# Mixer 1 of a two-layer hybrid backbone: second copies of context keys on VectorE, a dummy exponential, a query product placed inside the first attention, and norm steps pinned in TensorE's order

## The chip, the cores and the metric

The kernel runs on one core of one Trainium2 chip. TensorE (PE) multiplies matrices, VectorE (DVE), ScalarE (ACT) and GpSimd (POOL) work on their results, and SyncE (SP) and the others start DMA transfers. The metric is the device time of one execution in microseconds (us). Times are given as the median of several runs; the profile is that of one further execution, with its own time.

## The reference

A stream of 512 latent tokens and one of 256 context tokens, 1024 wide, pass two layers. Each layer is half a feed-forward network (FFN, SwiGLU, 2816 wide), a token mixer, and again half an FFN; each of these is modulated (scale and shift from a conditioning vector) and closed by a LayerNorm over the 1024 features of a token. The change lies in the mixer of the second layer, "mixer 1", and in the norm that closes the FFN ahead of it. Cut to what matters:

```
def layer_norm(x, g, b):
    mu = mean(x); var = mean(square(x - mu))
    return (x - mu) * rsqrt(var + LN_EPS) * g + b

def window_gqa(u_lat, u_ctx, w_qkv, w_o, sinks, with_ctx_out):
    # 16 query heads, 4 key/value heads, 64 wide; 512 latent rows in 4 blocks of 128; 256 context rows
    q = axial_rope(u_lat @ w_q) * scale          # (512, 16 heads, 64)
    k = axial_rope(u_lat @ w_k)                  # (512, 4 heads, 64)
    v = u_lat @ w_v
    kc, vc = u_ctx @ w_k, u_ctx @ w_v            # context keys: no rotation
    for b in range(4):                           # block of 128 queries against 3 blocks of keys
        s_win = where(|pos_q - pos_k| <= 128, q_b . k[b-1..b+1], -1e30)
        s_ctx = q_b . kc
        p = softmax([s_win, s_ctx, sink])        # sink: a logit per head without a value
        o_b = p_win @ v[b-1..b+1] + p_ctx @ vc
    return o @ w_o
```

Inputs and output are fp32.

## The kernel before, in words

**Precision.** Activations lie transposed: 1024 features in 8 tiles (k = 0 to 7) of 128 partitions, tokens along the free axis; columns 0 to 511 are latent tokens, 512 to 767 context. A matrix product is made of three products of the reduced type fp32r: each operand is a high part and the rest. `mm3` issues them: high by high (line 163), high by low (L165), low by high (L166). A weight quarter of 128x512 is split as it arrives: ScalarE makes the high part `wh` (L102), GpSimd the rest `wl` (L104). The modulated activations are `uh` and `ul` (L319, L321 and L323 on ScalarE, with a subtraction on VectorE).

**What sets the order.** Each engine runs its instructions in a fixed order and waits by semaphores for the others. The program text gives an order; the tile framework's scheduler, started with a timeline simulation (L1549), then reorders each engine's instructions within what their data allow. Two devices in the text steer it. `behind(x, y)` makes x stand after y on the same engine, without a wait. `plan(point=[steps])` puts steps into an agenda, and `at(point)` runs them at that point of the text: this is how the eight steps of a LayerNorm are spread over the product loop that comes next. `layer_norm(..., firm=True)` adds one more tie: the matmul after the variance product is put behind it, through the variable `in_front`, which `mm3` reads once and clears.

**The norm ahead of mixer 1** is called l3 and has a latent part l3[0] and a context part l3[1]. Its steps are sums, mean (matmul `pml`), centers (subtraction, squares on ScalarE L460, sums to `aql` on VectorE L356), variance (`pvl`, four or two small matmuls, L476), reciprocal root, spreading (`prl`, L404), and the last scaling and modulation. The steps of l3[1] are hung into mixer 1's first product loop at the points wa_3, wa_6 and wq0_0_4.

**Mixer 1** (`wa_mixer`) begins with one loop over the eight k tiles: for each k four value products `vw` (128x256, for four blocks of 128 tokens) and two key products `wk` (128x512, two key heads each) and the point `wa_k`. The key products are copied out with a scale (`qek`, L1125 on ScalarE) and rotated by `turned`: a matmul with a rotation matrix (`prk`, L1131), two VectorE operations (L1133, L1135) and one on GpSimd (L1134). `stack_k` then writes each key head into two tiles, so that high and low parts lie in the two halves of the partitions: a copy to its own half (L869, ScalarE), a copy to the other half (L870, ScalarE), the difference (L871, VectorE), and a copy of the difference (L872, ScalarE). It does this for the 512 latent columns and, later, for the 256 context columns (product `wkc`). Query products are `wq{u}_{i}` (u = 0 to 3, i = 0 or 1, two heads each; 8 k, so 24 products of 128x512); they are copied out with the scale (`qeq`, L1125), rotated (`prq`, L1131) and stacked by `stack_q` (L862 on ScalarE, L863 on VectorE). The text has this order: query 0_0, key rotations, query 0_1, rotation of query 0_0, context keys 0, rotation of query 0_1, context keys 1, context values (`vw_4` and `vw_5`), query 1_0, and then the attention of head pair 0.

**Attention** (`attn`) goes over four blocks of 128 queries. For each block and each of two heads the scores against the window (`sw`) and the context (`sc`) are two matmuls each (L877 high, L878 low part of the keys). VectorE adds the mask and takes the minimum (scores are negated) in two passes (L1221, L1224). ScalarE makes the exponentials with their sums (L1236, L1238, L1240). VectorE adds the sink's share (L1246 or L1249) and takes the reciprocal (L1250); GpSimd scales by it (L920). PE transposes the probabilities (`tpw`, `tpc`, L901), which are copied out, and multiplies them with the values (`wo`, L911). The points wm{s}_{b} and wo{s}_{b} lie after the transposes and at the end of block b of head pair s. After head pair 0 query 1_0 is rotated, and after head pair 1 query 1_1 is made.

## Time and profile before

| | |
|---|---|
| median of 3 runs | 2719.22 us (2715.05 to 2722.56) |
| profiled execution | 2723.84 us, its span 2722.1 us |
| mean granted TensorE clock | 0.991 |
| instructions | 47725 |
| PE busy, 0 to 2060 us | 2015.00 us, clock 1.00 |
| PE busy, 2060 to 2066 us | 6.00 us, clock 1.00 |
| PE busy, 2066 to 2122 us (start of mixer 1) | 51.72 of 56.00 us, clock 0.94 |
| PE busy, 2122 to 2722 us | 559.85 of 600.00 us, clock 0.98 |

The span runs from the first to the last instruction of the profiled execution; its time includes what lies around that. In the rows of the timeline the first number is the instruction's start in us from the span's start, the second its duration (of a group of xN together), then the engine, the line and operation, output and inputs, shapes, and in brackets the time for which the engine had stood idle before it and the instruction that ended the wait. In the rows of stages the first number after the window is its length; then come the busy times of PE, of the weight load, of VectorE, ScalarE and GpSimd, each with its count of instructions, and at the end PE's granted clock (1.00 is full), the DMA share and GB/s. Names lose their numbers there: `wq` is any of the query products, `sw` any window score.

### The profile page before, as it was taken

What the parts mean: (1) busy time and instruction counts of PE and PEld (TensorE: products, weight loads), DVE (VectorE), ACT (ScalarE), POOL (GpSimd) and SP (SyncE); (2) the same over time, 40 slices, a digit from 0 to 9 for tenths busy, and PEclk for the clock granted to TensorE, in tenths of its full rate; (3) what the DMA queues carried; (4) which work ended last, traced back from release to release, by engine and by line L of the source; (5) the groups of instructions that cost most, each with busy time, mean ns of one, the idle gap of its engine ahead of it and who ended that gap; (6) DMA issues with size and microseconds to landing.
All of it is one profiled execution on the core that took longest, in us unless ns stands there. A gap on an engine that the chain in (4) does not pass through costs nothing.

```text
span 2722.1 us, 47725 instructions
## 1 busy us (share of the span) xinstructions
PE 2632.6 (97%) x16858; PEld 2406.2 (88%) x16858; DVE 1835.4 (67%) x4268; ACT 1206.5 (44%) x2505; POOL 1666.3 (61%) x1515
## 2 busy tenths in 40 slices
PE   8999999999999899999999999999999998999997
PEld 5899998888888889999998899999987777899997
DVE  4977778775545687656565766666667776687765
ACT  5334343266455444443432534333327655554542
POOL 4786766455433566967664578676645544667762
PEclk9999999999999999999999999999999999999998
DMA  9367565522221213444453225546642111245551
GB/s 331 101 181 204 139 164 141 146 78 80 59 59 53 69 47 94 120 125 128 120 137 102 77 78 151 146 126 189 179 148 65 32 32 43 67 106 128 136 146 57
DMA packets 295758, 311.90 MB, mean 115 GB/s; under 512 B 27872, under 2 KB 194016, under 8 KB 294496
## 3 DMA queue, kind: packets, MB, share of 16 engines
q1 hardware_dynamic: 279104, 279.36, 35.0%
q0 software_dynamic: 16128, 29.37, 6.4%
q8 instruction: 133, 2.18, 0.3%
q14 instruction: 105, 0.86, 0.1%
q10 hardware_dynamic: 288, 0.14, 0.0%
HBM read 300.92 MB, written 12.25 MB: 115 GB/s over the span
## 4 chain that ended last, share of the span: by engine, by line
PE 55%; DVE 6%; ACT 1%; DMA 1%; issue 1%; POOL 0%; SPq 0%; DVEq 0%; ACTq 0%; POOLq 0%
PE pd0b L163 2%; PE pd0b L165 2%; PE pd0b L166 2%; PE pd1a L163 2%; PE pd1a L165 2%; PE pd1a L166 2%; PE wo L911 1%; DMA wr<-in_wst_dram 1%; PE pd1b L163 1%; PE pd1b L165 1%; PE pd1b L166 1%; DVE z L504 1%; PE tpw L901 1%; DVE sw L1221 1%; PE wq L163 0%
## 5 line engine op out<-in xcount | busy, mean ns | idle before, releaser
L104 POOL TENSOR_TENSOR wl<-wr,wh 128x512 fp32r<-128x512 f32 x200 | 261.9, 1327 | 148.4 <-ACT wh L102 95.2
L104 POOL TENSOR_TENSOR wl_s<-S,wh_s 128x512 fp32r<-128x512 f32 x240 | 318.1, 1361 | 54.4 <-ACT wh_s L102 53.9
L102 ACT CAST wh_s<-S 128x512 fp32r<-128x512 f32 x256 | 155.6, 621 | 426.9 <-POOL S L645 138.7
L645 POOL TENSOR_TENSOR S<-wr,wr 128x512 f32<-128x512 f32 x128 | 174.1, 1360 | 187.8 <-DMA wr<-in_wst_dram 165.4
L212 DVE CUSTOM_DVE_ANT_0 jk<-wt,cb 128x512 f32<-128x512 f32 x360 | 244.8, 680 | 21.6 <-DMA wt<-in_wmodt_dram 17.5
L104 POOL TENSOR_TENSOR wl_a<-wr,wh_a 128x512 fp32r<-128x512 f32 x144 | 190.0, 1366 | 19.3 <-ACT wh_a L102 16.9
L102 ACT CAST wh_a<-wr 128x512 fp32r<-128x512 f32 x192 | 119.1, 622 | 150.7 <-PE pd1b L165 19.4
L102 ACT CAST wh<-wr 128x512 fp32r<-128x512 f32 x200 | 120.8, 617 | 98.6 <-DMA wr<-in_wst_dram 18.9
L504 DVE SCALAR_TENSOR_TENSOR z<-pd0b,gt,z 128x256 f32<-128x256 f32 (+1 forms) x168 | 96.9, 594 | 39.3 <-PE pd0b L166 39.1
L504 DVE SCALAR_TENSOR_TENSOR z<-pd1a,gt,z 128x512 f32<-128x512 f32 (+1 forms) x150 | 88.9, 605 | 40.2 <-PE pd1a L166 39.1
L920 POOL TENSOR_SCALAR p<-p,l 128x512 f32<-128x512 f32 x64 | 44.5, 698 | 100.6 <-DVE l L1027 93.5
L504 DVE SCALAR_TENSOR_TENSOR z<-pd0a,gt,z 128x512 f32<-128x512 f32 (+1 forms) x160 | 93.8, 612 | 16.5 <-PE pd0a L166 16.2
L645 POOL TENSOR_TENSOR S<-wr,S 128x512 f32<-128x512 f32 x64 | 90.6, 1415 | 3.4
L645 POOL TENSOR_TENSOR S<-S,wr 128x512 f32<-128x512 f32 x64 | 90.1, 1408 | 2.9
L920 POOL TENSOR_SCALAR pw<-pw,l 128x512 f32<-128x512 f32 (+1 forms) x64 | 42.8, 670 | 72.2 <-DVE l L1250 42.2
L340 POOL TENSOR_SCALAR z<-z,ag_None,ab_None 128x256 f32<-128x256 f32 (+1 forms) x69 | 52.3, 762 | 51.7 <-DVE uh L325 32.6
L1026 ACT ACTIVATE p<-s,m 128x512 f32<-128x512 f32 x64 | 44.0, 689 | 77.8 <-DVE m L1023 73.4
L326 DVE TENSOR_TENSOR ul<-ufl,uh 128x256 fp32r<-128x256 f32 (+1 forms) x88 | 59.6, 685 | 6.1 <-ACT uh L321 3.1
L504 DVE SCALAR_TENSOR_TENSOR z<-pd1b,gt,z 128x512 f32<-128x512 f32 (+1 forms) x91 | 53.2, 618 | 10.0 <-PE pd1b L166 9.7
L319 ACT ACTIVATE ufl<-z,bi_None,sc_None 128x256 f32<-128x256 f32 (+1 forms) x77 | 48.1, 638 | 25.6 <-DVE z L489 25.2
L104 DVE TENSOR_TENSOR wl_a<-wr,wh_a 128x512 fp32r<-128x512 f32 x48 | 52.3, 1101 | 5.7 <-ACT wh_a L102 5.4
L163 PE MATMUL vn<-wh,uh 128*128 128x256 f32 x192 | 54.7, 285 | 1.1 <-DVE nq L863 0.6
(1483 smaller groups left out, 10583.5 us busy)
## 6 DMA issues: line engine op xcount, KB each, us to landing
wr<-in_wst_dram SPq DMA_DIRECT2D x456, 256.0 KB
wt<-in_wmodt_dram SPq DMA_DIRECT2D x206, 256.0 KB
wr_0b<-in_wst_dram SPq DMA_DIRECT2D x47, 256.0 KB
wr_1b<-in_wst_dram SPq DMA_DIRECT2D x47, 256.0 KB
wr_2b<-in_wst_dram SPq DMA_DIRECT2D x47, 256.0 KB
wr_3b<-in_wst_dram SPq DMA_DIRECT2D x47, 256.0 KB
wm<-in_wmod_dram SPq DMA_DIRECT2D x8, 1024.0 KB
zspare<-in_wmodt_dram SPq DMA_DIRECT2D x30, 256.0 KB
```

The lines of the kernel that those rows point to most:

```text
L102: nc.scalar.copy(hi[:], src[:])
L104: x = eng.tensor_tensor(out=lo[:], in0=src[:], in1=hi[:].bitcast(F32), op=ALU.subtract)
L163: behind(nc.tensor.matmul(ps, a[0], b[0], start=first, stop=False), in_front[0])
L165: nc.tensor.matmul(ps, a[0], b[1], start=False, stop=False)
L166: last_pe[0] = nc.tensor.matmul(ps, a[1], b[0], start=False, stop=last)
L212: x = nc.vector.tensor_tensor_reduce(out=junk[:], in0=w[:], in1=cb[st], scale=1.0, scalar=0.0, op0=ALU.mult, op1=ALU.add, accum_out=out[st])
L319: nc.scalar.activation(uv, zs, AF.Identity, scale=s1, bias=s2)
L326: return hi, nc.vector.tensor_tensor(out=lo, in0=uv, in1=uo.bitcast(F32), op=ALU.subtract)
L340: nc.gpsimd.tensor_scalar(out=zs, in0=zs, scalar1=prm[2][:, d:d + 1], scalar2=prm[3][:, d:d + 1], op0=ALU.mult, op1=ALU.add)
L504: last[0] = nc.vector.scalar_tensor_tensor(out=zt(d, c0, c1), in0=pd, scalar=gt[:, d, st:st + 1], in1=zt(d, c0, c1), op0=ALU.mult, op1=ALU ...
L645: nc.gpsimd.tensor_tensor(out=t[:], in0=a[:], in1=b[:], op=o)
L920: nc.gpsimd.tensor_scalar(out=p, in0=p, scalar1=r, scalar2=0.0, op0=ALU.mult, op1=ALU.add)
```

## The change

The change has four parts. One: for the context columns, `stack_k` makes the second copy (other half, L870) on VectorE and not on ScalarE. Two: after the copies out of the keys, an exponential of two columns of `nsink` (the negated sink logits, an input that is loaded at the start) is written to a small tile that nothing reads. Three: the product of query 1_0 is no longer in the text ahead of the attention but at the point wm0_0, in the first block of head pair 0, after that block's transposes. Four: a flag `sticky`, set at the point wa_6 and cleared at wq0_1, keeps `in_front` from being cleared, so that every product triple that is issued in between is put behind the norm's small matmul (L476 or L404 by which was last); and the last steps of l3[1] move from wq0_0_4 to wq0_0_7.

```diff
--- before.py
+++ after.py
@@ -157,11 +157,11 @@
         for f in agenda.pop(point, ()):
             f()
 
-    in_front = [None]
+    in_front, sticky = [None], [False]
 
     def mm3(ps, a, b, first, last):
         behind(nc.tensor.matmul(ps, a[0], b[0], start=first, stop=False), in_front[0])
-        in_front[0] = None
+        in_front[0] = in_front[0] if sticky[0] else None
         nc.tensor.matmul(ps, a[0], b[1], start=False, stop=False)
         last_pe[0] = nc.tensor.matmul(ps, a[1], b[0], start=False, stop=last)
 
@@ -863,11 +863,11 @@
             nc.vector.scalar_tensor_tensor(out=q[lo, c0:c1], in0=src[hi, :], scalar=scale, in1=q[hi, c0:c1].bitcast(F32),
                                            op0=ALU.mult, op1=ALU.subtract)
 
-    def stack_k(k0, k1, kl0, kl1, c0, c1, src):
+    def stack_k(k0, k1, kl0, kl1, c0, c1, src, both=False):
 
         for k, kl, own, other in ((k0, kl0, LOW, HIGH), (k1, kl1, HIGH, LOW)):
             nc.scalar.copy(k[own, c0:c1], src[own, :])
-            nc.scalar.copy(k[other, c0:c1], src[own, :])
+            (nc.vector.tensor_copy if both else nc.scalar.copy)(k[other, c0:c1], src[own, :])
             nc.vector.tensor_tensor(out=kl[own, c0:c1], in0=src[own, :], in1=k[own, c0:c1].bitcast(F32), op=ALU.subtract)
             x = nc.scalar.copy(kl[other, c0:c1], kl[own, c0:c1].bitcast(F32))
         return x
@@ -1154,6 +1154,7 @@
             at(f"wa_{k}")
         ks = [[slab(f"wk{x}_{i}") for x in ("0", "1", "l0", "l1")] for i in range(2)]
         kes = [scaled(f"k{i}", kp[i], 1.0) for i in range(2)]
+        nc.scalar.activation(small("le", "le_w"), nsink[:, 0:2], AF.Exp)
         vt = []
         for j in range(4):
             vt.append(vtile(f"vtw_{j}"))
@@ -1187,12 +1188,12 @@
             mmk(ps[:, :NC], w, i * P, NL, NT)
             if i == 0:
                 qs.append(stacked_q("q0_1", qes[1], "mm"))
-            last_k[0] = stack_k(*ks[i], NL, NT, ps[:, :NC])
+            last_k[0] = stack_k(*ks[i], NL, NT, ps[:, :NC], True)
         wv = wunit(again=iv)
         for j in (4, 5):
             context_v(j)
-        wq = wunit()
-        early = query(1, wq, 0, "ln")
+        wq, early = wunit(), []
+        plan(wm0_0=[lambda: early.append(query(1, wq, 0, "ln"))])
 
         def attn(s, q, oh, ol, bs=range(4), tags=("t", "mm")):
             kp = s // 4
@@ -1277,7 +1278,7 @@
             for i in range(2):
                 attn(u * 2 + i, qs[i], *[t[:, 0:NL] for t in os[i]])
                 if u == 0 and i == 0:
-                    early = stacked_q("q1_0", early)
+                    early = stacked_q("q1_0", early[0])
             qs = proj(u + 1) if u else [early, stacked_q("q1_1", query(1, wq, 1))]
             wo_pairs(f"w{u}", wunit(), os, [(0, NL, 0)], gt, ("mm",))
         os = o_tiles(3)
@@ -1418,7 +1419,10 @@
     gemv_dve(1, (24, 40, (0, 1)), (40, 72, (0,)))
     plan(pa1a_0_0_0=l2[0][6:], pa1a_0_1_0=l2[1][1:3], pd1a_0_0_1=l2[1][3:4], pd1a_0_0_4=l2[1][4:])
     ffn("1a", g2, lambda: gate(1, 2, 0.5), None, whole(l3[0], l3[1][:1]), apart=True)
-    plan(wa_3=l3[1][1:3], wa_6=l3[1][3:4], wq0_0_4=l3[1][4:6], wq0_1=l3[0][6:])
+    def stay(x):
+        sticky[0] = x
+
+    plan(wa_3=l3[1][1:3], wa_6=[lambda: stay(True)] + l3[1][3:4], wq0_0_7=l3[1][4:6], wq0_1=l3[0][6:] + [lambda: stay(False)])
     plan(wo6_2=l4[0][:1], wo6_3=l4[0][1:2], wm7_3=l4[0][2:3], wo7_3=l4[0][3:4] + [lambda: back(last_rstd[0])],
          pow3_1_256_2=[lambda: back(None)] + l4[0][4:6], pow3_1_256_7=l4[1][:1])
     wa_mixer(gate(1, 5, 1.0))
```

Line numbers in the changed kernel are one higher from the dummy exponential on (L1157), and L1236 becomes L1237. The places in the built order that follow are those of which the prediction speaks. A row is a line, an operation, the output, its inputs and the shape; numbers at the end of a name tell instances apart.

ScalarE at the beginning of the program, where the modulation vectors of layer 0 are made: `gev` is a copy of a conditioning product, `uh` the first FFN's activations, `wh` weight casts. This is a piece of the difference:

```order
 L321 CAST uh_106<-ufin_360 128x512
 L188 COPY gev_3_403<-gm_3_394 128x512
+L1157 ACT_TABLE_LOAD
+L1157 ACTIVATE le_w<-nsink 128x2
 L102 CAST wh_1_232<-wr_1_230 128x512
 L102 CAST wh_2_238<-wr_2_236 128x512
```

The dummy exponential and a table load ahead of it stand here; a little further on a second table load (L236) is added ahead of the copies `cb`. In mixer 1 the table load ahead of the first exponential stands in both kernels.

ScalarE at the start of mixer 1, a piece of the difference (`prk` is a rotated key, `qeq_0` the copy out of query 0_0, `ufl` and `uh` the context's modulated activations):

```order
-L102 CAST wh_3_23081<-wr_3_23079 128x512
-L869 CAST wk_0_23041<-prk_23155 64x512
-L870 CAST wk_0_23041<-prk_23155 64x512
+L1125 ACTIVATE qeq_0_23155<-wq_0_23087 128x512
+L869 CAST wk_0_23041<-prk_23157 64x512
+L870 CAST wk_0_23041<-prk_23157 64x512
+L319 ACTIVATE ufl_1_0_23116<-z_92,bi_0_1_3_None,sc_0_1_3_None 128x256
+L319 ACTIVATE ufl_1_1_23121<-z_93,bi_0_1_3_None,sc_0_1_3_None 128x256
+L323 ACTIVATE uh_102<-z_93,bi_0_1_3_None,sc_0_1_3_None 128x256
```

The copy out of query 0_0 now stands ahead of the first key copies; before, it stood behind them. On PE the two key rotations `prk` come after 20 of the 24 products of query 0_0, where before they came after 15, with 15 products of query 0_0 behind the norm's variance; and `pvl` of l3[1] stands ahead of all 18 products of the last k of the value and key loop, where before it came after 15 of them.

PE at the end of the mixer's projections, before the change: the last products of query 1_0, then the first scores of the attention.

```order
L163 MATMUL wq_0_23406<-uh_108,wh_3_23402 128x512
L165 MATMUL wq_0_23406<-ul_116,wh_3_23402 128x512
L166 MATMUL wq_0_23406<-uh_108,wl_3_23403 128x512
L877 MATMUL sc_1_0_23496<-wk_0_23041,wq_0_0_23216 128x256
L878 MATMUL sc_1_0_23496<-wkl_0_23043,wq_0_0_23216 128x256
L877 MATMUL sc_1_1_23504<-wk_0_23042,wq_0_1_23217 128x256
```

PE in the changed kernel a little later, where the same product now begins (`sw` window scores of block 1, `tpw` the transposes of block 0):

```order
L877 MATMUL sw_1_0_23495<-wk_0_23041,wq_0_0_23218 128x384
L878 MATMUL sw_1_0_23495<-wkl_0_23043,wq_0_0_23218 128x384
L877 MATMUL sw_1_1_23503<-wk_0_23042,wq_0_1_23219 128x384
L878 MATMUL sw_1_1_23503<-wkl_0_23044,wq_0_1_23219 128x384
L901 MATMUL tpw_0_0_23440<-idn,pw_0_0_23431 128x128 x4
L163 MATMUL wq_0_23455<-uh_101,wh_0_23386 128x512
L165 MATMUL wq_0_23455<-ul_109,wh_0_23386 128x512
L166 MATMUL wq_0_23455<-uh_101,wl_0_23387 128x512
```

The scores now follow directly on the last context value product `vw_5`, and query 1_0 stands behind the transposes of block 0's first head.

## The prediction

> **What bounds the kernel now.** I read the page's busy shares first, then TensorE's waits over the whole run, then the waits and the stage table of the piece that the change touches (mixer 1's start, 2065 to 2121 us), then each engine's timeline there.
>
> ```profile
> PE 2632.6 (97%) x16858; PEld 2406.2 (88%) x16858; DVE 1835.4 (67%) x4268; ACT 1206.5 (44%) x2505; POOL 1666.3 (61%) x1515
> PE sw L877 <- ACT pw L1236: 10.9, 13, 3.2
> PE sw L877 <- ACT pw L1236: 4.0, 3, 3.2
> ...
> 2072.06:2078.18 6.12, 6.12 (x29) 4.80 (x28) 3.77 (x9) 5.24 (x9) 3.06 (x3) 1.00 0.16 43
> 2078.18:2102.31 24.13, 23.87 (x150) 20.93 (x149) 18.59 (x34) 22.92 (x47) 17.15 (x13) 1.00 0.45 119
> 2103.00:2106.20 3.20, 0.04 (x1) 0.05 (x1) 1.36 (x6) 2.16 (x5) 0.00 (x0) 1.00 0.14 49
> 2108.20:2114.90 6.70, 6.11 (x33) 5.30 (x33) 4.73 (x19) 5.80 (x22) 3.72 (x7) 0.50 0.00 0
> 2114.90:2121.00 6.10, 6.10 (x61) 5.71 (x61) 4.29 (x19) 2.88 (x8) 1.84 (x4) 0.99 0.01 3
> ```
>
> The first row: TensorE (PE) works 97% of the span, so a gain can only be a stop of PE that is closed, and an added stop is paid in full. The second and third rows are PE's waits for the exponential, in the run and between 2100 and 2122 us: 4.0 of 10.9 us lie at the first attention block. The other rows are stages (length, then busy time of PE, weight load, VectorE, ScalarE, GpSimd, then PE's granted clock). PE stands still from 2103.0 to 2106.2, and then runs at half clock from 2108.2 to 2114.9: 6.11 busy us at 0.50, so about 3.1 us more lost. That hole, 3.2 + 0.24 + 0.59 us of waiting and 3.1 us of slow clock, is all that the change can win here. The two stages ahead of it show the cause to come: ScalarE is busy 22.92 of 24.13 us up to 2102.31.
>
> ```profile
> 2101.37 0.28 PE L877 MATMUL sc<-wk,wq 128*128 128x256 f32 x1
> 2102.68 0.28 PE L878 MATMUL sw<-wkl,wq 128*128 128x256 f32 x1
> 2106.16 0.44 PE L877 MATMUL sw<-wk,wq 128*128 128x384 f32 x1 [3.20 <-ACT pw L1236]
> 2107.60 0.66 PE L901 MATMUL tpw<-idn,pw 128*128 128x128 f32 x4
> 2108.84 0.69 PE L877 MATMUL sw<-wk,wq 128*128 128x384 f32 x1 [0.59 <-ACT pw L1236]
> 2121.01 1.02 PE L1131 MATMUL prq<-qeq,rm_sb 128*128 128x512 f32 x2
> 2101.03 0.37 ACT L870 CAST wk<-wkc 64x256 fp32r<-64x256 f32 x1
> 2101.43 0.88 ACT L872 CAST wkl<-wkl 64x256 fp32r<-64x256 f32 x2
> 2104.03 1.28 ACT L1236 ACT_TABLE_LOAD   x1 [1.10 <-DVE m L1224]
> 2105.32 0.69 ACT L1236 ACTIVATE pw<-sw,m 128x512 f32<-128x512 f32 x1
> ```
>
> The chain: first scores end at 2102.96, the table load starts at 2104.03, the exponential at 2105.32, PE goes on at 2106.16, and the first transposes (L901) at 2107.60. From 2121.01 (the rotation of the moved query product) PE's order is the same before and after until the next FFN, so I work out when PE gets there.
>
> **The dummy exponential.** It reads only nsink, and the built order puts it at about 41 us, not in the mixer; ScalarE then loads the silu table again (L236), and still loads the exponential's table in the first attention block. So the 1.28 us load of the row above stays, and two loads and an activation are added early.
>
> ```profile
> 41.45 2.19 ACT L102 CAST wh<-wr 128x512 fp32r<-128x512 f32 x4
> 47.27 2.51 ACT L319 ACTIVATE ufin<-z,mod,scNone_None 128x512 f32<-128x512 f32 x4 [3.63 <-DVE scNone_None L268]
> 52.24 1.11 ACT L236 ACTIVATE cb<-cr 128x512 f32<-128x512 f32 x2
> 54.94 0.60 ACT L531 ACTIVATE sl0a<-pa0a 128x512 f32<-128x512 f32 x1 [1.58 <-PE pa0a L166]
> ```
>
> At 41.45 about 1.28 + 0.3 us is put ahead of four weight casts; the 3.63 us in which ScalarE waits before 47.27 hide it. At 52.24 the 1.28 us fits in the 1.58 us of waiting before 54.94. I take 0; without that cover it is 2.9 us. By the Trainium skill ("ScalarE: Activation LUTs", What ACT_TABLE_LOAD costs) a switch costs about 2.66 us with its drain, which would make this 5.3 us uncovered; the trace has the exponential starting 1.29 us after the load, so no drain shows.
>
> **The norm steps pinned.** The variance product pvl (L476) now stands ahead of all 18 products of the last k in the first key/value stage; before, 15 of them ran first.
>
> ```profile
> 2067.11 0.42 DVE L356 TENSOR_TENSOR aql<-pml,sql 128x256 f32<-128x256 f32 x1
> 2065.63 0.28 PE L163 MATMUL vw<-wh,uh 128*128 128x256 f32 x1
> 2068.09 0.50 PE L476 MATMUL pvl<-onesd,aql 128*128 128x1 f32 x4
> 2068.45 0.37 PE L163 MATMUL vw<-wh,uh 128*128 128x256 f32 x1
> 2068.90 1.02 PE L1131 MATMUL prk<-qek,rm_sb 128*128 128x512 f32 x2
> 2069.99 0.39 PE L165 MATMUL wq<-ul,wh 128*128 128x512 f32 x1
> 2095.79 0.50 PE L163 MATMUL wq<-uh,wh 128*128 128x512 f32 x1 [0.26 <-DVE wq L863]
> ```
>
> Its input is ready at 2067.11 + 0.42 = 2067.53, but PE is there at 2065.63: it stops 1.9 us, with all later products queued behind. pvl takes 0.36 (2068.09 to 2068.45), the 18 products 2.46 + 0.45; this stage ends at 2067.53 + 0.36 + 2.9 = 2070.8 instead of 2068.90. The stop gains nothing further on: VectorE's small norm steps had their result before PE used it already. Below zero is excluded, since PE's work ahead is unchanged; above, 1.9 us is the whole distance.
>
> **The keys are rotated later, and ScalarE falls behind.** Because query product 0 is no longer interrupted after five k, the key rotations (L1131) come after 20 of its 24 products, and on ScalarE its copy out (qeq_0) stands ahead of the first key copies. A 512-wide product takes (2101.37 - 2095.79)/24 = 0.233 us, a rotation (2069.99 - 2068.90) - 0.23 = 0.86. So query product 0 is done at 2070.8 + 5.6 + 2 x 0.86 = 2078.1, and only then ScalarE starts on the keys. Before, it had done 5.24 us of that queue between 2072.06 and 2078.18. From 2078.1 it has that and the 22.92 us that followed, less the four context copies moved to VectorE (4 x 0.37): 2078.1 + 5.24 + 22.92 - 1.48 = 2104.8, where before it was done at 2102.31. Bounds: 2099.6 if no key work moves (24.13 less 1.21 us idle, less 1.48), 2106.0 if it also idles 1.21 us as before; I take 2104.8, since the order names the copies. The moved copies themselves cost nothing on VectorE: it is idle 5.5 us of those 24.13; they win 1.5 us on ScalarE, which is in the sum.
>
> **The query product moved.** Its 24 products hid the key copies before (2095.79 to 2101.37). Now PE reaches the first scores with nothing to do and waits for the copies. Block 0 needs all but ScalarE's last (0.40 us): 2104.4, and five products follow, so its scores end about 2105.2 (before 2102.96). ScalarE can load the table at about 2105.0 (before 2104.03), so PE goes on at 2107.1. VectorE's reciprocal now stands behind the masked minimum of the next block's scores:
>
> ```profile
> 2106.51 0.16 DVE L1250 RECIPROCAL l<-l 128x1 f32<-128x1 f32 x1
> 2106.81 0.63 DVE L1221 CUSTOM_DVE_ANT_0 sw<-sw,mk,nsink 128x384 f32<-128x384 f32 x1
> ```
>
> The product that it now follows takes 0.61 us on PE, the minimum 0.63 and its read 0.14, so the reciprocal starts at 2107.1 + 1.4 = 2108.5, 2.0 us later, and so do the transposes: 2109.6. And here is the point of the order: the moved product stands *behind* these transposes on PE, so the hole of 3.2 us isn't filled. It fills at most the 0.59 us before 2108.84. Everything from there to 2121.01 is PE work (the stage to 2114.9 at half clock, the next full), so the 5.6 us come on top.
>
> **Sum.** +2.0 (transposes later) + 5.6 (query product now in the open) - 0.6 (one wait filled) = +7.0 us, with as long a half clock as before. The few swapped rows in the next FFN I take as 0 (its waits are each under 2.2 us). The profiled execution is 2723.84 us, 1.7 over its span and 4.6 over the median 2719.22; so 2730.8 on its own scale, 2726.2 on that of the median.
>
> **The rivals.**
>
> *PE keeps full clock.* After the change PE's stops are shorter pieces (about 2 us each) between 2100 and 2110. If none lowers the clock, 3.1 us come off: +3.9, 2723. Against it:
>
> ```profile
> 948.00:950.00 2.00, 1.17 (x8) 0.76 (x6) 2.00 (x8) 0.78 (x2) 2.00 (x3) 1.00 0.00 0
> 950.00:952.00 2.00, 1.08 (x12) 1.08 (x14) 2.00 (x7) 0.00 (x0) 1.92 (x4) 0.77 0.00 0
> 952.00:954.00 2.00, 2.00 (x14) 1.67 (x11) 1.91 (x8) 1.12 (x3) 2.00 (x4) 0.50 0.04 8
> ```
>
> There 0.83 + 0.92 us of standing still were enough for a half clock. For it: the Trainium skill ("TensorE: Matmul & The Clock Gate", Part 1) has the throttle come after an idle window of about 3.4 us; by that rule this rival is the result. The rows at 948 us disagree with it.
>
> *Half clock twice or longer.* If the 1.9 us stop at 2065.6 also lowers the clock for some 3.4 us (half of 6.7), or the second period lasts one half longer, each costs 1.7 us: +8.7 to +10.4, 2729.
>
> *ScalarE is not the holder.* If the key copies are made in the idle time of the other steps and are ready when PE gets to the scores, it gets there at 2070.8 + 24 x 0.233 x 2 + 4 x 0.86 + 96 x 0.12 + 0.4 = 2097.3, 4.1 us before 2101.37; then the same 6.2 us to the transposes, 5.6 more, 0.6 filled, and with less waiting the full clock: -4.1 + 5.6 - 0.6 - 3.1 = -2.2, 2717. This is the only way to faster; it decides from where block 0's last key copy ends by about 2100.5 (3.9 us earlier than I have it), and the order on ScalarE speaks against it. (0.12 is the 256-wide step: nine of the 15 products between 2065.63 and 2068.09 are 256 wide, and (2.46 - 6 x 0.233)/9 = 0.12.)
>
> *Nothing moves.* Of the title's four parts the dummy doesn't do what it says; that is in the forecast. That the other three also leave the time (within 1 us) would need the late keys and the half clock to cancel: it lies between the cases above.
>
> **How the numbers follow.** A measurement of this kernel can tell about 0.3% (8.2 us) from no change. Forecast, +5.5 to +8.5: 0.45. Full clock, 2723: 0.23. Longer half clock, 2729: 0.22. ScalarE not the holder, 2717: 0.10. The predicted time is 2726. The range takes in the outer two and the spread of the runs (7.5 us over three): 2717 to 2732. Slower by over 0.3% is most of the longer half clock and a part of the forecast, 0.33; faster by over 0.3% only the tail of the last case, 0.04; the rest, 0.63, is within.
>
> **What would show it.** ScalarE: an exponential table load at 41 us, a silu load at 52, and one still ahead of the first attention's exponential. PE: an idle time of about 1.9 us before pvl; waits of the first scores (sc, sw) for L872 or L870 adding up to over 4 us; still 1.5 to 2.5 us before the 384-wide scores; wq1_0 behind the first transposes and none of it in a hole; the rotation prq about 7 us later than 2121. The forecast is wrong if the first scores don't wait for key copies, or if wq1_0 runs while PE waits for the exponential.

## The result, and the profile after

The changed kernel takes 2728.13 us (median of 9 runs, 2722.53 to 2734.88), the kernel before 2719.57 us (median of 9, 2713.17 to 2722.56): a ratio of 1.0031 with a 95% interval of 1.0018 to 1.0044, 8.6 us slower. Forecast were 2726 and a range of 2717 to 2732.

The two profiled executions differ by less (spans 2723.0 and 2722.1 us), because they reach mixer 1 at different times: its first value product starts at 2045.41 us before and at 2038.20 after. Over all profiles of this study that start lies between 2036 and 2048 us, whatever was changed behind it. So the profiles are compared from this product on. The "stage" is from it to the rotation (L1131) of the moved query product, from where PE's order is the same in both kernels until the next FFN. These are rows of PE's timeline before and, in the second fence, after:

```profile
2045.41 0.39 PE L163 MATMUL vw<-wh,uh 128*128 128x256 f32 x1 [1.25 <-ACT uh L321]
```

```profile
2038.20 0.39 PE L163 MATMUL vw<-wh,uh 128*128 128x256 f32 x1 [1.25 <-ACT uh L321]
2060.38 0.61 PE L476 MATMUL pvl<-onesd,aql 128*128 128x1 f32 x4 [1.80 <-DVE aql L356]
2087.02 0.38 PE L165 MATMUL wkc<-ul,wh 128*128 128x256 f32 x1 [1.09 <-DVE ul L326]
2093.33 0.28 PE L877 MATMUL sc<-wk,wq 128*128 128x256 f32 x1
2094.51 0.38 PE L878 MATMUL sc<-wkl,wq 128*128 128x256 f32 x1 [0.90 <-ACT wkl L872]
2097.93 0.58 PE L878 MATMUL sc<-wkl,wq 128*128 128x256 f32 x1 [1.31 <-ACT wkl L872]
2099.27 0.41 PE L878 MATMUL sw<-wkl,wq 128*128 128x256 f32 x1
2101.18 0.69 PE L877 MATMUL sw<-wk,wq 128*128 128x384 f32 x1 [1.49 <-ACT pw L1237]
2103.85 1.12 PE L901 MATMUL tpw<-idn,pw 128*128 128x128 f32 x4 [0.82 <-POOL pw L920]
2121.22 1.02 PE L1131 MATMUL prq<-qeq,rm_sb 128*128 128x512 f32 x2
```

The stage was 2121.01 - 2045.41 = 75.60 us and is 2121.22 - 2038.20 = 83.02: 7.4 us longer, most of the loss of 8.6 us in the time (by its interval, 4.9 to 12.0 us). PE's waits between 2055 and 2125 us in the changed kernel (in total, times, longest) show what is new: the stop ahead of pvl, waits for VectorE (`ul`, `wkl`), and the first scores' waits for key copies.

```profile
PE sc L878 <- ACT wkl L872: 2.2, 2, 1.3
PE pvl L476 <- DVE aql L356: 1.8, 1, 1.8
PE wkc L165 <- DVE ul L326: 1.8, 2, 1.1
PE sw L877 <- ACT pw L1237: 1.7, 2, 1.5
PE tpw L901 <- POOL pw L920: 0.8, 1, 0.8
PE vw L163 <- DVE wkl L871: 0.5, 1, 0.5
PE sc L877 <- DVE wk L870: 0.5, 1, 0.5
PE sw L877 <- DVE wkl L871: 0.2, 1, 0.2
```

ScalarE's timeline after the change:

```profile
41.26 1.28 ACT L1157 ACT_TABLE_LOAD   x1
52.16 1.28 ACT L236 ACT_TABLE_LOAD   x1
...
2071.14 0.60 ACT L1125 ACTIVATE qeq<-wq 128x512 f32<-128x512 f32 x1 [6.59 <-PE wq L166]
2098.38 0.41 ACT L872 CAST wkl<-wkl 64x256 fp32r<-64x256 f32 x1 [0.51 <-DVE wkl L871]
2099.05 1.28 ACT L1237 ACT_TABLE_LOAD   x1 [0.27 <-DVE m L1225]
```

The dummy's load stands at 41 us, a second one follows at 52, and the load in mixer 1 is still there. The copy out of query 0_0 now stands ahead of the keys on ScalarE, which waits 6.59 us for it. The key rotations follow the query on PE: they start 30.09 and 30.95 us into the stage, where before they started at 23.49 and 27.78. (Before, only the second of them stood behind 15 products of query 0_0, the first ahead of all; the description of the change puts both behind 15.) ScalarE's last key copy ends 60.59 us into the stage (2098.38 + 0.41 - 2038.20), where before it was 56.90 (2101.43 + 0.88 - 2045.41).

In the windows of the clock (columns as in the stage table of the profile before) PE runs at half clock for three windows of 3.41 us, where before it was two:

```profile
2093.25:2096.67 3.42, 1.83 (x10) 1.06 (x8) 1.96 (x5) 3.30 (x7) 3.09 (x3) 1.00 0.49 146
2096.67:2100.08 3.41, 1.76 (x5) 1.22 (x5) 2.49 (x8) 2.59 (x6) 1.88 (x2) 0.50 0.65 199
2100.08:2103.49 3.41, 1.86 (x4) 1.00 (x4) 2.15 (x11) 2.06 (x7) 0.38 (x1) 0.50 0.23 63
2103.49:2106.91 3.42, 3.06 (x10) 2.58 (x11) 1.87 (x10) 3.10 (x11) 2.03 (x4) 0.50 0.00 0
2106.91:2110.32 3.41, 3.41 (x19) 2.81 (x17) 0.36 (x2) 0.00 (x0) 1.04 (x2) 1.00 0.00 0
```

### The profile page after: what moved, and what is told of

Its sections match the earlier page's. It is cut to its first block, busy times and chain, and to the rows that moved or that the text cites. A ratio compares the mean times of both kernels' runs of the same rounds, so it can differ in the third digit from the quotient of the medians.

```text
span 2723.0 us, 47731 instructions
## 1 busy us (share of the span) xinstructions
PE 2629.8 (97%) x16858; PEld 2401.4 (88%) x16858; DVE 1823.0 (67%) x4272; ACT 1208.1 (44%) x2504; POOL 1663.4 (61%) x1515
## 4 chain that ended last, share of the span: by engine, by line
PE 54%; DVE 6%; DMA 2%; ACT 2%; issue 1%; POOL 1%; POOLq 0%; DVEq 0%; ACTq 0%; SPq 0%
PE pd0b L165 2%; PE pd0b L163 2%; PE pd0b L166 2%; PE pd1a L163 2%; PE pd1a L165 2%; PE pd1a L166 2%; DMA wr<-in_wst_dram 2%; PE pd1b L163 1%; PE pd1b L166 1%; PE pd1b L165 1%; PE wo L911 1%; DVE z L504 1%; DVE z L373 1%; PE tpw L901 1%; PE wq L163 1%
```

## The experiments

The theory (A): the pin stops PE and holds query 0_0 together, the keys are rotated later, ScalarE and VectorE are late with the key copies; the moved query no longer covers this, and stands itself behind the hole that it could have filled. The rivals: the moved query alone makes the loss (B), or the half clock does (C). The results are in one table; the times are ratios to the kernel before, measured beside each. "Low windows" are windows of 3.41 us at half clock within the stage. A stage is that of one execution. In the hole filled, the candidate and the query split PE's rows stand in another order around the stage's end, so their stages compare with the others only roughly.

| kernel | stage, us | low windows | ratio of times (95%) |
|---|---|---|---|
| before | 75.60 | 2 | 1 |
| before, second execution | 74.92 | 2 | (one run) |
| changed | 83.02 | 3 | 1.0031 (1.0018 to 1.0044) |
| pin alone | 79.86 | 2 | 1.0028 (1.0012 to 1.0044) |
| move alone | 79.92 | 4 | 1.0014 (0.9997 to 1.0031) |
| copies alone | 74.87 | 2 | 0.9993 (0.9977 to 1.0010) |
| hole filled | 74.52 | 0 | 0.9994 (0.9976 to 1.0012) |
| changed, without pin | 77.66 | 3 | 1.0009 (0.9993 to 1.0026) |
| changed, without move | 78.39 | 1 | 1.0033 (1.0014 to 1.0052) |
| changed, pin without its stop | 77.66 | 3 | 1.0016 (1.0002 to 1.0030) |
| changed, order in the FFN restored | 84.85 | 4 | 1.0024 (1.0004 to 1.0044) |
| late dummy | 73.48 | 1 | 0.9984 (0.9971 to 0.9998) |
| candidate | 75.58 | 2 | 1.0010 (0.9991 to 1.0030) |
| query split | 71.30 | 0 | 0.9984 (0.9968 to 1.0000) |

**Pin alone, move alone, copies alone.** Each is the kernel before with one part of the change's diff: the `sticky` lines and the two moved points; the `wm0_0` lines; the `both` lines.

> Before plus only the pinned norm steps (part four). 'Stage' is the time on PE from the mixer's first value product (vw) to the rotation of the moved query product (prq); it is 75.6 us before and 83.0 after. Theory A (the prediction's chain: the pin's stop of about 1.8 us, then keys rotated later and ScalarE late with the key copies): laying the trace's durations on the built order gives +3.7 us, stage about 79.3, time +3 to +5; the first scores start about 4 us later than before although query 1_0 still stands ahead of them. Theory B (the pin costs only its own stop, the rest of the loss is the moved query): stage +1.8, about 77.4. Theory C (the loss is mostly a longer half clock that the added stops bring on): stage +1.8 and the clock still at 0.50 for about 6.7 us, or longer by what the stage exceeds 77.4.

> Before plus only the moved query product (part three). Theory A: without its cover the scores come earlier (about 2097 to 2100 instead of 2101.4, waiting for key copies), the query's 5.6 us stand in the open behind the first transposes: +2.9 us by the trace's durations on the built order, stage about 78.5, time +2 to +4. Theory B (the moved query makes most of the change's loss): stage +5.6 or more, 81 to 83. Theory C (the clock): as A, but the half clock lies elsewhere and its length decides by up to 3 us either way: 75.5 to 81.5, and PE's granted clock shows it.

> Before plus only the second context key copies on VectorE (part one). Theory A: ScalarE is through with the keys about 1.1 us sooner, but the first scores stand behind query 1_0, whose end (2101.4) sets them: stage 75.6 within 0.3, time within 2 us of before. If ScalarE's key copies were what the first scores of the kernel before waited for, the stage would be about 1 us shorter.

The pin costs 4.3 us in the stage and the moved query 4.3 as well, the key copies nothing that the second execution of before (74.92) doesn't show too. Both figures hold a share of the clock, as C allowed. Of the pin alone A had 3.7; one of its low windows follows on the stop, with PE busy throughout, and costs half of 3.41 us, 1.7 us. Of the move alone A had 2.9; it ran four low windows. B falls all the same: with the pin alone the first transposes begin 68.49 us into the stage (62.19 before), and 6.3 - 1.7 = 4.6 us is far more than the stop of 1.8. But the path is A's only in part: no score waits for a key copy here. PE's own waits for VectorE make most of it, 1.80 + 1.08 + 0.68 + 0.47 = 4.0 us, the stop and then the context activations (`ul`) and a key's rest:

```profile
2060.01 0.61 PE L476 MATMUL pvl<-onesd,aql 128*128 128x1 f32 x4 [1.80 <-DVE aql L356]
2088.20 0.39 PE L165 MATMUL wkc<-ul,wh 128*128 128x256 f32 x1 [1.08 <-DVE ul L326]
2090.22 0.39 PE L165 MATMUL wkc<-ul,wh 128*128 128x256 f32 x1 [0.68 <-DVE ul L326]
2091.55 0.38 PE L163 MATMUL vw<-wh_0b,uh 128*128 128x256 f32 x1 [0.47 <-DVE wkl L871]
```

And PE's timeline of the move alone shows the scores without their cover, waiting for VectorE's copy of a value product and for a key copy of ScalarE:

```profile
2098.41 0.35 PE L877 MATMUL sc<-wk,wq 128*128 128x256 f32 x1 [1.99 <-DVE vtw L852]
2100.58 0.58 PE L878 MATMUL sc<-wkl,wq 128*128 128x256 f32 x1 [1.82 <-ACT wkl L872]
2106.41 0.69 PE L877 MATMUL sw<-wk,wq 128*128 128x384 f32 x1 [2.23 <-ACT pw L1236]
```

**Without the pin, without the move.** The changed kernel with these parts undone.

> The changed kernel with part four undone (norm steps as before); dummy, key copies and moved query stay. Stage as in the first runs (first vw to the rotation of the moved query): 75.6 before, 83.0 after; pin alone 79.9, move alone 79.9. Theory A (one chain: late key copies are paid only because the query no longer covers them, so the parts overlap): laying the trace's durations on the built order gives +1.8 at full clock, and the longer half clock of the moved query alone (13 us instead of 7) adds up to 1.5: stage 77.4 to 79, no wait before pvl, the first scores waiting under 2 us for key copies. Theory B (the parts are independent and add up): 83.0 - 4.3 = 78.7, or 79.9 less nothing for the copies. Time +2 to +4 by either; the clear mark is the waits.

> The changed kernel with part three undone: query 1_0 ahead of the attention again; pin, dummy and copies stay. Theory A: stage +3.8 at full clock, 79.4 (range 79 to 80), the first scores about 4 to 6 us later than before and none waiting for a key copy, since query 1_0 covers them; PE still stops about 1.8 us before pvl and another 1.8 us for the context activations. Theory B (independent parts): 83.0 - 4.3 = 78.7. Should the stage come out at 82 or more, the moved query costs nothing by itself and the pin is the whole loss.

Without the pin the stage is 2.1 us over before, without the move 2.8, both parts together 7.4. The 2.5 us that are missing need no meeting of late copies with uncovered scores: they come from where the low windows lie. The first transposes and the rotation that ends the stage, without the move and then without the pin:

```profile
2104.32 1.06 PE L901 MATMUL tpw<-idn,pw 128*128 128x128 f32 x4
2115.66 1.02 PE L1131 MATMUL prq<-qeq,rm_sb 128*128 128x512 f32 x2
2099.23 1.05 PE L901 MATMUL tpw<-idn,pw 128*128 128x128 f32 x4
2116.12 1.02 PE L1131 MATMUL prq<-qeq,rm_sb 128*128 128x512 f32 x2
```

Cut at the transposes, the stage has these two pieces (in us, the first counted from the first value product; the last column takes half of the time at half clock off the second piece):

| kernel | to the transposes | from there to the rotation | of this at half clock | without its loss |
|---|---|---|---|---|
| before | 62.19 | 13.41 | 6.83 | 10.0 |
| changed, without move | 67.05 | 11.34 | 2.54 | 10.1 |
| changed, without pin | 60.77 | 16.89 | 2.12 | 15.8 |
| changed | 65.65 | 17.37 | 3.06 | 15.8 |

Up to the transposes the pin costs 4.9 us with the move and without it, and the move wins 1.4 us with the pin and without it (both kernels in between have the key copies on VectorE too, which alone change little: 62.41 us). Behind them the move costs 5.8 us either way, once the half clock is taken off. So these parts add up, 4.9 - 1.4 + 5.8 = 9.3, and the changed kernel pays 7.4 because 1.9 us less is lost there to the half clock. The other kernels with these rows, or nearly these, agree: 9.8 to 10.5 us with the query ahead of the attention (before again, copies alone, pin alone, late dummy), 15.8 with it behind the transposes (move alone, pin without its stop, order in the FFN restored). For the kernel without the pin A's bounds for the stage hold; without the move A had 79 to 80, and 78.4 lies nearer to B's 78.7.

**The pin without its stop.** `sticky` is set at the next point:

```diff
-    plan(wa_3=l3[1][1:3], wa_6=[lambda: stay(True)] + l3[1][3:4], wq0_0_7=l3[1][4:6], wq0_1=l3[0][6:] + [lambda: stay(False)])
+    plan(wa_3=l3[1][1:3], wa_6=l3[1][3:4], wa_7=[lambda: stay(True)], wq0_0_7=l3[1][4:6], wq0_1=l3[0][6:] + [lambda: stay(False)])
```

> The changed kernel with the pin set one point later (wa_7 instead of wa_6), so that the norm's small variance product isn't pinned ahead of the last 18 products; the spreading product stays pinned and its steps stay at wq0_0_7. Theory A (the stop of 1.8 us, and the late key rotations that it brings by holding query 0_0 back, are the pin's whole loss): no wait before pvl, the rotations as in before, stage 77.7 to 78.5, as without the pin at all (77.66). Rival (the moved spreading and its pin make the rotations late): stage 80 to 83.

77.66, as without any pin, with the transposes at 60.66 us (60.77 without any pin), no wait before pvl and the rotations at 23.50 and 28.47. So the pin's loss in the stage comes from pvl ahead of the last 18 products, by the stop and what it makes late, and none that shows from the pinned spreading or its later point.

**The hole filled with waste.** Twelve products that nobody reads, behind the first block's scores (`last_sc` is the last score matmul):

```diff
+                if s == 0 and b == 0:
+                    spare_ps = bank("c", "spare")
+                    for n in range(12):
+                        behind(nc.tensor.matmul(spare_ps[:], uh[0][:, 0:P], uh[1][:, 0:NL], start=True, stop=True), last_sc[0])
```

> Before plus twelve products of 128x512 (uh by uh, into a free bank, read by nobody: pure waste, 2.7 us of PE work) behind the first block's scores, in the hole of 3.2 us in which PE waits for the exponential. Nothing else is changed and the output is the same. If the hole is what brings the half clock (6.7 us at 0.50 before, 3.1 us lost): the clock stays at 1.00 to 2121, and the stage gets 2.8 us shorter (3.1 less 0.3 for a wait that ends a little later), 72.8, time -2 to -3, although PE does more. If the half clock comes from something else (the later waits, the load on the chip): stage 75.6 to 76, time the same or +0.3.

```profile
2104.79 2.92 PE L1234 MATMUL spare<-uh,uh 128*128 128x512 f32 x12
2108.15 0.44 PE L877 MATMUL sw<-wk,wq 128*128 128x384 f32 x1 [0.21 <-ACT pw L1240]
2109.00 0.45 PE L877 MATMUL sw<-wk,wq 128*128 128x384 f32 x1 [0.24 <-ACT pw L1240]
2110.65 0.65 PE L901 MATMUL tpw<-idn,pw 128*128 128x128 f32 x4 [0.36 <-POOL pw L920]
2112.08 0.45 PE L877 MATMUL sw<-wk,wq 128*128 128x384 f32 x1 [0.78 <-ACT pw L1240]
```

The clock stayed at 1.00 through the stage, as expected of the hole as its cause. But only 1.1 us came of it against the one execution of before and 0.4 against the other, not 2.8: PE waits for exponentials and scaling instead (0.21, 0.24, 0.36, 0.78 us). This doesn't price the half clock of before, since the scheduler put PE's scores and transposes behind the filler in another order. In the order of before the table above shows half of the low time as lost, between 2.5 and 6.8 us of it; no run has that order with none. And at 2130.76 the clock fell at the next hole, which took the gain back (to the rotation of query 1_1 103.09 us against 102.42).

**The order in the next FFN.** In the changed kernel PE waits for 1.93 us at the start of a group of that FFN:

```profile
2350.01 0.60 PE L404 MATMUL prl<-idn,yl 128*128 128x128 f32 x4
2352.55 0.50 PE L163 MATMUL pa1b<-uh,wh 128*128 128x256 f32 x1 [1.93 <-ACT uh L321]
```

Before has no such wait. In the built order the norm's spreading product (L404) stands behind 18 more matmuls of the output product (`pd1b`) there, because VectorE's steps of the reciprocal root are mixed with sums. This experiment ties them together again:

```diff
-    plan(pa1b_0_0_0=l4[0][6:] + l4[1][1:3], pv1b_0_1_0=l4[1][3:4], pd1b_0_0_3=l4[1][4:])
+    plan(pa1b_0_0_0=l4[0][6:] + l4[1][1:3], pv1b_0_1_0=l4[1][3:4], pd1b_0_0_2=l4[1][4:] + [lambda: back(last_rstd[0])], pd1b_0_0_7=[lambda: back(None)])
```

> The changed kernel with one thing added: in the FFN behind mixer 1 the reciprocal root of norm l4[1] is tied together on VectorE (its last steps at pd1b_0_0_2 and later sums behind it), so that TensorE's order there is that of before; mixer 1 is untouched. Theory A (besides its 7.4 us in mixer 1 the change loses about 1.9 us by a swapped place of the norm's spreading product in that FFN, the wait of 1.9 us of pa1b for uh): stage 83.0 as in the changed kernel, within 1.7 us by half-clock windows; the wait of 1.9 us gone; time 1 to 2 us less than the changed kernel, +6 to +8 against before. Rival (the swapped rows cost nothing, the wait is made up later): time +8.6 as the changed kernel.

The 1.9 us wait is gone from the trace. The stage of this execution was 84.85 with four low windows, one of them brought on by the pin's stop; in the stage the rows of all engines are those of the changed kernel in the same order, so the 1.8 us over 83.02 belong to this execution, and that window, with PE busy throughout, accounts for 1.7 of them. The time (1.0024, 1.0004 to 1.0044) can't be told from the changed kernel's: that the wait costs its 1.9 us in the time is not shown. In pin alone and in the change without the move this FFN has the same wait and another 1.4 us for `ul`, which with their stages comes near their times (pin alone: 4.3 + 1.9 + 1.4 = 7.6 us, and 0.28% of 2719.89 is 7.6). With an interval of 3.3 to 12 us for that time, and a stage that chance moves by 1.8, this agreement proves little.

**A dummy that can't be hoisted.** It reads a key's rest, which is written just ahead of the attention:

```diff
+            if i == 0:
+                nc.scalar.activation(small("le", "le_w")[LOW, :], ks[0][3][LOW, NL:NL + 2].bitcast(F32), AF.Exp)
```

> Before plus a dummy exponential that can't be hoisted: it reads two columns of the first context key's rest (written by ScalarE a little ahead of the attention), so that the table load (1.28 us) is made there and none stands ahead of the first attention's exponential. Theory A (the load is on the chain scores, minimum, load, exponential): PE's wait of 3.2 us gets about 1.2 us shorter, stage 74.4; if the shorter wait leaves the clock at 1.00, as the filled hole did, 73.3. Rival: the load, put ahead of the second key's copies on ScalarE, delays something that the first scores need: stage 75.6 or more. Time -1 to -2.5 by A.

```profile
2092.90 1.28 ACT L1192 ACT_TABLE_LOAD   x1
2095.47 0.69 ACT L1238 ACTIVATE pw<-sw,m 128x512 f32<-128x512 f32 x1
```

Now the load runs while PE computes the first scores, and PE's wait is 2.25 us instead of 3.20: that is the 0.95 us that the load costs on the chain. The stage is 2.1 us shorter (1.4 against the second execution), with one low window instead of two; the rest lies behind the transposes, where 3.41 us ran at half clock for 6.83.

**Two ways to fill the hole with work.** The candidate puts the last context value product behind the first scores, at a new point `ws` that stands after a block's scores, beside copies on VectorE, the late dummy and another bank for query 1_0:

```diff
-        for j in (4, 5):
-            context_v(j)
+        context_v(4)
+
+        def fill():
+            in_front[0] = last_sc[0]
+            context_v(5)
+
+        plan(ws0_0=[fill])
...
-        early = query(1, wq, 0, "ln")
+        early = query(1, wq, 0, "ln", "c")
...
+                at(f"ws{s}_{b}")
```

> A version meant to fill the hole with work that has to be done: before plus key copies on VectorE, plus the late dummy, plus the product of query 1_0 in a bank of tag c, so that it need not wait for the rotation's bank, plus the last context value product vw_5 (24 products of 256, 2.9 us) behind the first block's scores. No pin, query ahead of the attention. Theory A: laying the trace's durations on the built order gives -2.4 us at full clock, stage 73.2; with the clock at 1.00 throughout, as with the filled hole, another 1: 72.2. Time -2 to -4. Rival: filling the hole gains nothing, since the chain of exponential, reciprocal and transposes on the other engines sets the pace to 2121 (the filled hole won 1.1 only): stage 74.5 to 75.6.

The rival held: 75.58, two low windows, and no gain in time. The value product takes 2.9 us where the wait was shorter, PE's waits for exponentials follow it (1.30 and 0.23 us in the stage), and this kernel has the 1.9 us wait of the FFN as well. The second version has copies on VectorE and the late dummy as well, leaves vw_5 and the bank as they were, splits query 1_0 (`product` issues its triples for some k into one bank), and restores the order in the FFN as above:

```diff
-        early = query(1, wq, 0, "ln")
+        def rest():
+            in_front[0] = last_sc[0]
+            product(range(6, DT))
+            early.append(scaled("q1_0", half, -0.125, "ln"))
+
+        product(range(6))
+        plan(ws0_0=[rest])
```

> A version for both ends: before plus key copies on VectorE, plus the late dummy, plus query 1_0 cut in two (18 of its 24 products ahead of the first block's scores, the last 6, 1.4 us, behind them, in the hole), and in the next FFN the norm's reciprocal root kept together on VectorE by an order tie, so that TensorE's rows there stand as before. Since other rows change places around the moved query's rotation, the stage is taken to the rotation of query 1_1: 102.42 us before, 109.58 after, 100.29 with the late dummy alone. Theory A (chain of scores, minimum, exponential starts earlier, and the hole is filled with real work): -2.8 at full clock by the trace's durations on the built order, 99.6, up to 1.7 us either way by where half-clock windows fall; time -2 to -4 against before and not slower than the late dummy. Rival (as in the candidate: the chain on the other engines sets the pace, filling gains nothing): 100.3 to 102.4, time as the late dummy or as before.

To the rotation of query 1_1 it took 98.79 us (expected 99.6, before 102.42), and no window was low. PE's windows show that no stretch of the place is half idle any more:

```profile
2088.00:2092.00 4.00, 4.00 (x22) 3.41 (x21) 3.83 (x8) 3.36 (x10) 4.00 (x4) 1.00 0.71 189
2092.00:2096.00 4.00, 3.18 (x16) 2.06 (x15) 2.82 (x12) 3.39 (x8) 0.50 (x2) 1.00 0.51 165
2096.00:2100.00 4.00, 3.05 (x16) 2.09 (x16) 3.64 (x17) 3.50 (x14) 1.28 (x2) 1.00 0.00 0
2100.00:2104.00 4.00, 3.85 (x40) 3.43 (x39) 3.37 (x15) 3.05 (x12) 2.93 (x6) 1.00 0.00 0
```

Its time is 0.9984 (0.9968 to 1.0000), as that of the late dummy (0.9984, 0.9971 to 0.9998). Their intervals lie wholly below that of the changed kernel. Against the kernel before both gain about 4 us, the late dummy just outside its interval's chance, the split query at its edge. That the split gains anything over the late dummy alone is not shown: its 98.79 us against 100.29 are 1.5 us, and the late dummy's one low window accounts for up to 1.7.

**The kernel before, once more.**

> The kernel before once more, to see how far one execution's stage differs from another's. If the half clock goes by windows of 3.41 us, as the profiles so far suggest (low stretches of 3.41, 6.83, 10.24 or 13.65 us, following on a window with PE busy under about half), then the same waits fall otherwise into the windows: stage 75.6 within 1.7 us (73.9 to 77.3), low for a whole number of windows. If the half clock is set by the program alone: 75.6 within 0.1, low from 62.8 to 69.6 us behind the first vw as before.

Stage 74.92, low from 2102.78 to 2109.60, or 60.9 to 67.7 us behind the first vw, where the first execution had 62.8 to 69.6: the windows fell otherwise. An execution's stage can so differ by 0.7 us with nothing changed, and by 1.8 us between the changed kernel and the one with the FFN's order restored, whose rows in the stage are the same. Differences of stages below about 1.8 us show nothing unless the windows are told apart, as in the table of the two pieces.

## Why the prediction was right, point by point

The forecast's sum was +7.0 us; the stage shows +7.4, the time +8.6. The mechanism was right: in the changed kernel the first scores do wait for late key copies, and the moved query stands in the open. That the number came so near is in part luck, since two terms were wrong in opposite directions.

- **The dummy: right.** Loads at 41.26 and 52.16, and the one in the mixer kept (2099.05).
- **The pin's stop: right**, 1.80 us for 1.9.
- **Keys late on ScalarE: right in kind, too small.** Its last key copy came 2.5 us later by the sum and 3.7 in the trace, which is the prediction's own upper bound (2106.0 against 2102.31). The sum counted ScalarE's queue alone; VectorE was late as well, with the differences that ScalarE copies (0.51 us of waiting ahead of the last one) and with the context activations (PE's 1.8 us for `ul`), which the prediction had nowhere.
- **The scores and the transposes: too small.** Block 0's scores ended 3.9 us later into the stage (2.2 expected), the transposes began 3.5 us later (65.65 against 62.19 us; 2.0 expected).
- **The query in the open, 5.6 - 0.6: right but for the clock.** From the transposes to the rotation it added 4.0 us (17.37 against 13.41), not 5.0. Without the loss to half clock it added 5.8: nothing of it was hidden. The step "with as long a half clock as before" failed: before, both low windows lay behind the transposes; after the change there were three, but they lay mostly ahead of them, in the waits, and only 3.06 us were left behind. (6.83 - 3.06) / 2 is 1.9 us less. So 0.8 too little for the query and 1.9 us that the clock gave back make a term that is 1.0 too large; the transposes' error of 1.5 us the other way nearly cancelled it. That is luck: another execution with the same rows in the stage (the kernel with the FFN's order restored) took 84.85 us, 9.2 more than before.
- **The swapped rows in the next FFN, taken as 0: wrong.** They show a wait of 1.93 us; its part in the time could not be shown.
- **The expected sign "waits of the first scores of over 4 us" failed**: 2.7 us for ScalarE's and VectorE's key copies (L872, L870), since PE itself came later, held up by VectorE.

Of the rivals, "full clock" fell: the changed kernel ran three low windows, though its stops were shorter pieces. Its price of 3.1 us for the half clock of before is borne out as far as the runs reach: in the order of before, the piece behind the transposes took 13.41 us with 6.83 us at half clock and 12.47 with 5.37 (copies alone), and 11.34 with 2.54 without the move, so half of the low time is lost. "Longer half clock" was partly right: the pin's stop does bring on a low window in some executions (pin alone, and the change with its FFN order restored), and the changed kernel had three windows for two. "ScalarE not the holder" fell by the waits on L872 (0.90 and 1.31 us).

The hardware rule weighed in the prediction (the Trainium skill, "TensorE: Matmul & The Clock Gate", Part 1) speaks of a throttle after an idle window of about 3.4 us. By that rule, as the prediction used it, the changed kernel should have kept full clock; it had 10.24 us of half clock after a window in which PE was busy 1.83 of 3.42 us. The length of the window agrees, the condition does not.

## What to carry to other kernels

An order tie that puts a small dependent product ahead of a long run of ready ones stops the engine for the whole distance to its input, and what stands behind it shifts the copies on two other engines: count the work that the tie moves, not only the wait that it makes. A product that covers late copies and could also fill a hole behind them can do both when it is cut in two; moved whole past the hole, as here, it does neither. A dummy that shall preload a table needs an input that comes into being where the load is to stand; with an input that is ready early the scheduler put it at 41 us here. Before parts of a change are called dependent because their stages don't add up, take the half clock off each piece.

## What the hardware showed that was not expected

The half clock comes in windows. In each profile all changes of the clock lie whole numbers of 3.413 us apart, and low stretches last one, two, three or four windows, or, at the end of the program, till its end. Whether a window is low goes mostly by the one ahead of it. These are windows of the pin alone, cut at the clock's own edges: PE is busy 1.61 of 3.41 us around the stop, and the next window is at 0.50 though PE is busy throughout.

```profile
2057.84:2061.25 3.41, 1.61 (x12) 1.24 (x11) 2.22 (x7) 1.39 (x4) 0.00 (x0) 1.00 0.17 46
2061.25:2064.66 3.41, 3.41 (x13) 2.94 (x12) 1.98 (x10) 1.82 (x4) 1.18 (x1) 0.50 0.01 2
```

Over the 14 profiles, of the windows at full clock in which PE was busy less than 0.40, all 36 were followed by a low one; of those from 0.40 to 0.50, 21 of 28; from 0.50 to 0.55, 28 of 53; above that, 2 of some ten thousand. This leaves out the first 20 us, where 27 windows below 0.40 had no low one behind them, and the last low stretch of each profile, which follows on a window with PE busy between 0.64 and 0.91; why these differ is open. Behind a low window in which PE was busy throughout the clock came back in 67 of 75 cases; behind one busy 0.85 or less, in none of 27. The edges lie differently in each execution: the second execution of before had its hole almost whole in one window (busy 0.22 of 3.42 us), the first had it spread over two, and both ran two low windows.

```profile
2099.36:2102.78 3.42, 0.22 (x2) 0.13 (x2) 1.47 (x8) 2.26 (x6) 0.00 (x0) 1.00 0.13 43
2102.78:2106.19 3.41, 3.14 (x10) 2.18 (x11) 2.72 (x12) 2.13 (x9) 1.38 (x2) 0.50 0.00 0
```

So whether a hole of about half a window lowers the clock depends on where the edges fall, and a part of the scatter between executions is likely this: the pin's stop was followed by a low window in the pin alone and in the change with its FFN order restored, and not in the changed kernel.
